# A two-block transformer on one core: the residual spilled to DRAM during the experts, and the second context stream woven in at 1.65 instead of 1.1

## The chip, the cores and the metric

The kernel runs on one core of one Trainium2 chip. The metric is the device time of one execution in microseconds (us): the median of three runs. The engines are named as the profile names them: PE (TensorE matmul), PEld (TensorE weight load), DVE (VectorE), ACT (ScalarE), POOL (GpSimd) and SP (SyncE, which only issues DMAs here).

## The reference

Two transformer blocks run one after the other on 512 latent tokens of width 1024. The first block ends in a mixture of experts, and the second block has two layers, each with its own context stream of 256 tokens. Cut to what matters:

```
# block 1
x = x + gt1 * token_mixer(...)                       # 512 x 1024
h2 = modulate(rms_norm(x, norm_ffn_g), sh2, sc2)
x = x + gt2 * hier_moe(h2)     # 32 experts, top-2 of 8 in the top-1 of 4 groups
x = rms_norm(x, final_norm_g)
# each expert: (silu(h @ w_gate) * (h @ w_up)) @ w_down, 1024 -> 512 -> 1024

# block 2, layer 0 and 1
for i in range(2):
    # keys and values of ctx_2 (256 tokens) and of x (512 tokens), three branches, merge, MLP
    x_new = x + gt1 * mix(x, ctx) + gt2 * squared_relu_mlp(...)
    if i == 0: ctx = ctx + ... mix_c ... + squared_relu_mlp(...)   # needs ctx_2 alone, not x
```

The context stream of layer 0 depends on `ctx_2` and on the second block's weights, and not on the output of the first block. It can therefore run beside the experts.

## The kernel before

All data are float32. Most products are made from high and low parts (`split`, L167 to L169: ACT writes the high part, DVE the low part) as three matmuls (L192, L193, L194). The experts use plain float32 matmuls instead (L1015 for gate and up, L1034 for down).

**Streams and weaving.** The parts of the program are Python generators that yield a number, an estimate of the work just laid down. `weave` steps the stream whose own time is lowest, and a stream's time advances by its number over its `speed`. A `main` stream has speed 1. The context path of layer 0, `path(0, 256)`, is in the list `ctx` and goes along behind several main streams: behind the last attention head, `project`, `route`, `experts` and `combine`. For the last two its speed is `CTX_SPEED`. What is left of it then runs alone (`drain(weave(ctx))` in `run`), and after that comes the latent path, `path(0, 512)`. Weaving sets the order of the program text, which is a priority: when the program is built, each engine's instructions are put in a fixed order from these priorities and from when operands and buffers were expected to be ready. On the chip each engine runs its list in that order.

**Numbers of the streams.** One pair of experts yields 4.2 + 4.2 + 4.2 + 0.5 = 13.1, and 16 pairs 209.6. `combine` yields 4 + 4 + 8 + 8 x 1.5 = 28. Of the context path, the steps still to come when the experts begin yield 354 in all, of which its MLP (the last part) is 163.2.

**The experts.** 32 experts are done as 16 pairs. A pair computes 64 rows of two experts: `gu` takes 8 rounds, first 4 of gate, then 4 of up, then `hr` and `hT`, then `py` in 4 rounds. Each round uses two weight tiles of 128 x 1024 (512 KB), one of each expert, in eight matmul instructions of 128x512, which use 64 columns of the array each. So a pair has 24 tiles and 96 instructions: 32 for gate, 32 for up, 32 for down. The tiles have the tag `wa`, of which there are 14 buffers (`WA`). `branch` starts the first `EARLY` tiles before the experts; every other tile is loaded where it is used in program order, as soon as a buffer is free. All these loads are issued by SP (L152), in one queue with the context path's weights (`wr`, 4 buffers `raw`, then 6 buffers `hl` for their high and low parts).

**The residual.** `project` writes the residual X, eight tiles of 128x512 in four `wa` buffers. `route` reads it for the router's norm. X then stays in these four buffers during the experts, so that 10 are left for expert weights. `combine` gathers the experts' rows from DRAM (`yr`, L1048), adds them to X (L1058), takes the sum of squares (`stat`, L235, L237, L241; `rms`, L248), scales X (L1066), stores it in `xs_dram[0]` (L1067) and prepares the sum of squares of the next norm, which opens `path(0, 512)`.

**Context MLP.** It has four quarters, and each quarter has 192 matmuls on `f` (first product) and 192 on `u` (second product), 1,536 in all, with 128x256 outputs.

Of the kernel before, what the change touches and what calls it, by code (L numbers as in the profile page):

```python
# [16 lines left out]
KD = 8  # L17
# [5 lines left out]
NONE = 4096  # L23
LAMBDA_INIT = 0.8 - 0.6 * math.exp(-0.3 * 0)
T2, WA, RAW, HL, AT = 35, 14, 4, 6, 9
EARLY = 8
CTX_SPEED = 1.1
MOD_SPEED = 0.4
PRIOR = 30
FIRST = 70.0  # L30
# [48 lines left out]
def weave(main, back=()):  # L79


    every = list(main) + list(back)
    for s in every:
        s.t = 0.0
    while any(not s.done for s in main) or any(s.hold for s in every):
        live = [s for s in every if not s.done]
        held = [s for s in live if s.hold]
        if held:
            live = [s for s in live if s.hold or not s.weights]
        if all(s.done for s in main):  # L90
            live = held
        yield abs(min(live, key=lambda v: v.t).step())


def drain(gen):
    for _ in gen:
        pass
# [7 lines left out]
class Gen:  # L105
# [252 lines left out]
    def run(self):  # L358
# [42 lines left out]
        if one:  # L401
            for gen, speed, held in ((project, PRO_SPEED, True), (self.route(), ROUTE_SPEED, False), (None, 0, 0),
                                     (self.experts(), CTX_SPEED, False), (self.combine(), CTX_SPEED, False)):
                if gen is None:
                    self.branch()
                    continue
                for s in ctx:
                    s.speed = speed
                drain(weave([Stream(gen, 1.0, held, (lambda: tc.high_priority(PRIOR)) if PRIOR and held is not None and speed != CTX_SPEED else None)], ctx))
        if two:  # L410
# [371 lines left out]
    def route(self):  # L782
        nc, A, tc = self.nc, self.A, self.tc
# [3 lines left out]
        X = self.X  # L787
# [11 lines left out]
        def ct(shape, name):  # L799
# [8 lines left out]
        ps = self.mm("lgT")  # L808
        yield from self.norm_mod(X, a2, b2, 512, h2, self.ss, lambda k: nc.tensor.matmul(
            ps[:36], wr[:, k, :], h2[k], start=k == 0, stop=k == KD - 1))  # L810
        lT = self.at("lgT")[:, :512]
        nc.vector.tensor_copy(lT[:36], ps[:36])
        ps = self.tp("lg")
# [133 lines left out]
    def branch(self):  # L947
# [4 lines left out]
        self.wq = []  # L952
        for _ in range(EARLY):
            self.next_weights()
# [83 lines left out]
            yield 0.5  # L1038

    def combine(self):  # L1040
        nc, X, ss = self.nc, self.X, []
        gf = self.const("final_norm_g")

        Y = []
        for t in range(4):
            rows = [self.wa("yr") for _ in range(2)]
            for j in range(2):
                nc.gpsimd.indirect_dma_start(out=rows[j], out_offset=None, in_=self.Yd[:, :],  # L1048
                                             in_offset=bass.IndirectOffsetOnAxis(ap=self.rows_at[:, 4 * j + t:4 * j + t + 1], axis=0))
            self.copy_act(rows[0], rows[0], scale=self.wt[:, 0, t:t + 1])  # L1050
            nc.vector.scalar_tensor_tensor(rows[0], rows[1], self.wt[:, 1, t:t + 1], rows[0], op0=OP.mult, op1=OP.add)
            Y.append(rows[0])
        yield 4
        for m in range(KD):
            ps = self.tp("yT")
            for t in range(4):
                self.tr(ps[:, t * P:(t + 1) * P], Y[t][:, m * P:(m + 1) * P])
            nc.vector.scalar_tensor_tensor(X[m], ps, self.gt2[:, m:m + 1], X[m], op0=OP.mult, op1=OP.add)  # L1058
            self.stat(ss, m, X[m], 512)
        del Y  # L1060
        yield 4
        r = self.spread(self.rms(ss, 512), 512)
        yield 8
        ss = []
        for m in range(KD):
            nc.vector.scalar_tensor_tensor(X[m], X[m], gf[:, m:m + 1], r, op0=OP.mult, op1=OP.mult)  # L1066
            nc.gpsimd.dma_start(self.xs_dram[0][m], X[m])  # L1067
            self.stat(ss, m, X[m], 512)
            yield 1.5
        self.ss = ss  # L1070
# [822 lines left out]
```

## Time and profile before

| | us |
|---|---|
| time, median of 3 runs | 3581.45 (3577.01 to 3581.93) |
| time of the profiled execution | 3592.64 |
| its span, first to last instruction | 3590.9 |
| first expert matmul | 614.8 |
| last expert matmul ends | 1369.4 |
| sum of squares that opens the latent path | 1551.1 |
| latent path's first norm complete | 1568 |

PE is busy 95% of the span, PEld 71%, DVE 47%, ACT 34% and POOL 10%. A PE slice lasts longer than the distance to the next one, because matmuls are pipelined. So a busy PE need not be a PE at its peak; the distance from one start to the next tells that. The DMA engines move 165 GB/s over the span, and some 330 GB/s during the experts.

### The profile page before, as it was taken

What the parts mean: (1) busy time and instruction counts of PE and PEld (TensorE: products, weight loads), DVE (VectorE), ACT (ScalarE), POOL (GpSimd) and SP (SyncE); (2) the same over time, 40 slices, a digit from 0 to 9 for tenths busy, and PEclk for the clock granted to TensorE, in tenths of its full rate; (3) what the DMA queues carried; (4) which work ended last, traced back from release to release, by engine and by line L of the source; (5) the groups of instructions that cost most, each with busy time, mean ns of one, the idle gap of its engine ahead of it and who ended that gap; (6) DMA issues with size and microseconds to landing.
All of it is one profiled execution on the core that took longest, in us unless ns stands there. A gap on an engine that the chain in (4) does not pass through costs nothing. (4 is left out here: it accounts for less than half of the span.)

```text
span 3590.9 us, 48889 instructions
## 1 busy us (share of the span) xinstructions
PE 3407.6 (95%) x19280; PEld 2545.7 (71%) x19280; DVE 1698.4 (47%) x3173; ACT 1234.3 (34%) x2194; POOL 341.7 (10%) x402
## 2 busy tenths in 40 slices
PE   7999998999999997999999999999999999999999
PEld 4977556555455446998567777888897777778887
DVE  5336535323322325654346746444555466644443
ACT  4214313323222213433335433333434344423332
POOL 1000001011111102110000112000200001020000
PEclk9999999999999998999999999999999899999999
DMA  7231566998889885543752223333433221132232
GB/s 262 85 126 36 187 224 239 348 363 339 318 322 351 314 291 217 186 136 105 242 174 71 61 68 107 99 119 117 138 106 105 79 79 60 37 123 83 94 100 82
DMA packets 195667, 591.84 MB, mean 165 GB/s; under 512 B 31867, under 2 KB 36731, under 8 KB 195436
## 3 DMA queue, kind: packets, MB, share of 16 engines
q1 hardware_dynamic: 177308, 537.55, 43.6%
q0 software_dynamic: 18128, 51.15, 3.9%
q8 instruction: 152, 2.49, 0.3%
q14 instruction: 79, 0.65, 0.1%
HBM read 561.59 MB, written 31.20 MB: 165 GB/s over the span
## 5 line engine op out<-in xcount | busy, mean ns | idle before, releaser
L169 DVE TENSOR_TENSOR wl<-wr,wh 128x1024 fp32r<-128x1024 f32 (+2 forms) x452 | 555.9, 1234 | 502.5 <-ACT wh L168 485.1
L168 ACT ACTIVATE wh<-wr 128x1024 fp32r<-128x1024 f32 (+2 forms) x452 | 471.9, 1048 | 665.1 <-PE mm L193 495.4
L192 PE MATMUL mm<-wh,h 128*128 128x256 f32 (+1 forms) x1104 | 323.9, 294 | 7.7 <-ACT h L277 4.3
L193 PE MATMUL mm<-wl,h 128*128 128x256 f32 (+1 forms) x1104 | 320.8, 291 | 0.0
L194 PE MATMUL mm<-wh,h 128*128 128x256 f32 (+1 forms) x1104 | 319.9, 291 | 0.2
L192 PE MATMUL mm<-f,wh 128*128 128x512 f32 (+1 forms) x768 | 276.6, 362 | 8.7 <-ACT wh L168 5.0
L1015 PE MATMUL gu<-we,xT 128*64 128x512 f32 x1024 | 283.3, 605 | 0.9 <-ACT xT L165 0.7
L192 PE MATMUL mm<-u,wh 128*128 128x512 f32 (+1 forms) x768 | 274.4, 358 | 5.2 <-ACT wh L168 5.0
L194 PE MATMUL mm<-f,wl 128*128 128x512 f32 (+1 forms) x768 | 276.8, 361 | 1.6 <-DVE wl L169 1.6
L194 PE MATMUL mm<-u,wl 128*128 128x512 f32 (+1 forms) x768 | 274.3, 358 | 3.6 <-DVE wl L169 3.6
L193 PE MATMUL mm<-f,wh 128*128 128x512 f32 (+1 forms) x768 | 275.8, 360 | 0.0
L193 PE MATMUL mm<-u,wh 128*128 128x512 f32 (+1 forms) x768 | 273.6, 357 | 0.0
L192 PEld LDWEIGHTS mm<-wh,h 128*128 128x128 f32 x1104 | 218.8, 198 | 22.3 <-issue 9.0
L194 PEld LDWEIGHTS mm<-wh,h 128*128 128x128 f32 x1104 | 218.3, 198 | 6.7 <-issue 4.7
L193 PEld LDWEIGHTS mm<-wl,h 128*128 128x128 f32 x1104 | 219.1, 199 | 2.9 <-issue 2.3
L192 PE MATMUL pg<-h,wh 128*128 128x512 f32 (+1 forms) x576 | 212.3, 369 | 7.2 <-ACT th L1715 4.8
L194 PE MATMUL pg<-h,wl 128*128 128x512 f32 (+1 forms) x576 | 209.0, 363 | 0.6 <-DVE wl L169 0.6
L193 PE MATMUL pg<-h,wh 128*128 128x512 f32 (+1 forms) x576 | 208.8, 363 | 0.0
L355 ACT ACTIVATE p<-S,mx 128x768 f32<-128x768 f32 (+2 forms) x192 | 144.6, 756 | 115.4 <-DVE mx L1422 62.3
L192 PEld LDWEIGHTS mm<-f,wh 128*128 128x128 f32 x768 | 148.6, 194 | 38.0 <-ACT wh L168 7.9
L194 PEld LDWEIGHTS mm<-f,wl 128*128 128x128 f32 x768 | 148.2, 193 | 33.3 <-issue 9.7
L192 PEld LDWEIGHTS mm<-u,wh 128*128 128x128 f32 x768 | 147.3, 192 | 29.0 <-ACT wh L168 7.6
(504 smaller groups left out, 6420.9 us busy)
## 6 DMA issues: line engine op xcount, KB each, us to landing
wr<-in_ffn_w_dram SPq DMA_DIRECT2D x192, 512.0 KB, 3.8
wr<-in_w_in_dram SPq DMA_DIRECT2D x178, 512.0 KB, 4.3
we<-in_expert_w_gate_dram SPq DMA_DIRECT2D x128, 512.0 KB, 6.8
we<-in_expert_w_up_dram SPq DMA_DIRECT2D x128, 512.0 KB, 7.3
we<-in_expert_w_down_dram SPq DMA_DIRECT2D x128, 512.0 KB, 7.2
wm<-in_w_mod_dram SPq DMA_DIRECT2D x96, 256.0 KB, 5.6
wm<-in_w_mod_dram SPq DMA_DIRECT2D x48, 512.0 KB, 4.8
wm<-in_w_ada_dram SPq DMA_DIRECT2D x64, 256.0 KB, 4.7
```

What stands on the lines that cost most here:

```text
L168: self.nc.scalar.activation(hi, src, AF.Copy)
L169: self.nc.vector.tensor_tensor(lo, src, hi.bitcast(F32), op=OP.subtract)
L192: mm(out, ah, bh, start=i == 0, stop=False)
L193: mm(out, ah, bl, start=False, stop=False)
L194: mm(out, al, bh, start=False, stop=i == n - 1)
L355: self.nc.scalar.activation(p, s, AF.Exp, bias=m, accum_out=sm)
L1015: nc.tensor.matmul(gu[64 * e:64 * e + 64, m * 512:m * 512 + 512], xT[k // 4][:, o:o + 64], w[e][kk], start=k == 0, stop=k == KD - 1)
```

## The change

`EARLY` becomes 12 and `CTX_SPEED` 1.65. At the end of the router's norm the eight tiles of X are stored to `xs_dram[0]` by POOL, and the program lets go of them, so that all 14 `wa` buffers are open to the experts. `combine` loads X again through SP into four `wa` buffers.

```diff
-EARLY = 8
-CTX_SPEED = 1.1
+EARLY = 12
+CTX_SPEED = 1.65
...
         yield from self.norm_mod(X, a2, b2, 512, h2, self.ss, lambda k: nc.tensor.matmul(
             ps[:36], wr[:, k, :], h2[k], start=k == 0, stop=k == KD - 1))
+        for m in range(KD):
+            nc.gpsimd.dma_start(self.xs_dram[0][m], X[m])
+        del X
+        self.X = None
...
     def combine(self):
-        nc, X, ss = self.nc, self.X, []
+        nc, ss = self.nc, []
+        X = self.X = self.load_x(self.xs_dram[0], 512, "xr", "wa")
```

## Rows read from the trace of the kernel before

**Rows 1.** The page's part 1: busy time, share, instructions of each engine.
```profile
PE 3407.6 (95%) x19280; PEld 2545.7 (71%) x19280; DVE 1698.4 (47%) x3173; ACT 1234.3 (34%) x2194; POOL 341.7 (10%) x402
```
**Rows 2.** Windows: length, each engine's busy time and count, PEclk, DMA share, GB/s.
```profile
613.00:1369.40 756.40, 717.59 (x3748) 390.11 (x3748) 223.80 (x468) 194.95 (x391) 95.16 (x128) 0.97 0.88 329
1369.40:1551.00 181.60, 163.05 (x1254) 159.60 (x1253) 120.54 (x166) 80.15 (x113) 37.58 (x37) 0.92 0.57 191
1551.00:1567.50 16.50, 10.42 (x62) 9.27 (x61) 14.22 (x30) 6.32 (x9) 2.70 (x5) 0.69 0.45 152
```
**Rows 3.** Timeline, PE: a whole block of 32, then 48 context matmuls.
```profile
629.38 7.09 PE L1015 MATMUL gu<-we,xT 128*64 128x512 f32 x32
636.40 0.39 PE L192 MATMUL mm<-h,wh 128*128 128x256 f32 x1
...
642.26 0.60 PE L208 MATMUL ht<-cc,hr 128*128 128x128 f32 x4
```
**Rows 4.** Timeline, PE: a block taken in pieces between context matmuls.
```profile
1262.39 1.93 PE L1034 MATMUL py<-we,hT 128*64 128x512 f32 x6
1264.25 0.39 PE L193 MATMUL mm<-f,wh 128*128 128x256 f32 x1
...
1265.16 1.07 PE L1034 MATMUL py<-we,hT 128*64 128x512 f32 x2
1266.16 0.38 PE L193 MATMUL mm<-f,wh 128*128 128x256 f32 x1
```
**Rows 5.** Timeline, PE: the first and the last burst of just two expert matmuls.
```profile
714.01 1.07 PE L1015 MATMUL gu<-we,xT 128*64 128x512 f32 x2
...
1338.99 1.07 PE L1015 MATMUL gu<-we,xT 128*64 128x512 f32 x2
```
**Rows 6.** Waits of SP's queue, 613 to 1369: us in total, times, longest.
```profile
SPq L152 <- PE gu L1015: 289.3, 155, 13.8
SPq L152 <- PE py L1034: 170.8, 59, 15.1
```
**Rows 7.** Waits of PE, 613 to 1369.
```profile
PE mm L192 <- ACT wh L168: 11.7, 9, 1.7
...
PE gu L1015 <- DMA we<-in_expert_w_gate_dram: 0.3, 1, 0.3
```
**Rows 8.** Windows: the stretch in which the DMAs moved most.
```profile
750.00:800.00 50.00, 48.26 (x280) 28.15 (x277) 11.03 (x14) 10.80 (x16) 4.26 (x6) 1.00 0.99 377
```
**Rows 9.** Windows with one tile, PE alone: `f`, the context MLP's first product.
```profile
613.00:1369.40 756.40, 31.00 (x192) 0.97 0.88 329
```
**Rows 10.** The same for `u`, the second product.
```profile
613.00:1369.40 756.40, 22.05 (x144) 0.97 0.88 329
```
**Rows 11.** Timeline, all engines: the links of `combine` and the next norm.
```profile
1374.73 1.02 POOL L1048 DMA_INDIRECT yr<-Yd,cc  x1 [3.11 <-issue]
...
1396.08 1.28 DVE L1051 SCALAR_TENSOR_TENSOR yr<-yr,cc,yr 128x1024 f32<-128x1024 f32 x1
...
1413.54 0.59 PE L248 MATMUL ss<-cc,sq 128*128 128x1 f32 x2 [6.53 <-POOL sq L241]
...
1424.11 0.75 DVE L1066 SCALAR_TENSOR_TENSOR xr<-xr,cc,rb 128x512 f32<-128x512 f32 x1 [0.79 <-PE rb L208]
...
1441.89 0.73 DVE L1066 SCALAR_TENSOR_TENSOR xr<-xr,cc,rb 128x512 f32<-128x512 f32 x1
...
1551.10 1.84 PE L248 MATMUL ss<-cc,sq 128*128 128x1 f32 x16
```
**Rows 12.** Timeline, POOL: the idle stretch before the first store of the router's rows.
```profile
561.53 0.58 POOL L824 DMA_DIRECT2D Hd<-h2r  x1 [42.92 <-ACT h2r L165]
```
**Rows 13.** The page's part 6: DMAs, KB each, median us from issue to landing.
```profile
xres<-xr POOLq DMA_DIRECT2D x16, 256.0 KB, 3.4
xr<-xres SPq DMA_DIRECT2D x16, 256.0 KB, 5.3
```

## The prediction

> **What bounds the kernel now.** I read the page's busy times first, then windows by stage, then PE's timeline inside the experts. PE is busy 95% of the span [rows 1], so the question is where its time isn't work. The stage of the experts lasts 756.4 us with PE busy 717.6 us of them, but PEld only 390 us [rows 2]. The distances between starts tell more. A whole block of 32 expert matmuls takes 636.40 - 629.38 = 7.02 us, 0.219 us each, and the 48 context matmuls behind it take 5.86 us, 0.122 us each [rows 3]. At these paces the 1,536 expert matmuls (16 pairs of 96) need 337 us, and the other 3748 - 1536 = 2,212 need 270 us. That is 607 us; 149 us of the stage are lost.
>
> Where they go is seen in the second timeline. A round of eight expert matmuls is often cut in two and six, because one tile of the round was expected later than the other. The two halves of the array then don't work side by side: six take 1264.25 - 1262.39 = 1.86 us, two take 1.00 us [rows 4], and eight in a whole block 1.75 us. With the context run that is started once more between them (six matmuls in 0.91 us instead of 0.73), a cut costs 2.86 - 1.75 + 0.18 = 1.29 us. There are 52 bursts of exactly two in the stage, none before 714 us [rows 5], so cuts cost some 67 us. PE's clock stands at a mean of 0.97 in the stage [rows 2], which at its two levels means 45 us at 1.2 GHz and 23 us lost. The rest is the ends of short bursts and waits of PE for the high parts of context weights, the largest group 11.7 us; expert weights are hardly ever waited for, 0.3 us [rows 7].
>
> Why were the tiles expected late? SP waited 289 + 171 us for PE to free buffers [rows 6], so the ten buffers set how far ahead loads can run. The stage moved 329 GB/s x 756.4 us = 249 MB; at the paces above, in 607 us, it would need 410 GB/s. The busiest 50 us that I found in this stage moved 377 [rows 8]. So at full pace weights can't keep up, and the order was laid around that.
>
> The Trainium skill, Perfetto Trace Analysis, section Identifying the Most-Contended Engine, says that matmul busy time misjudges headroom and that LDWEIGHTS busy should be used. By the busy row, 95%, context work moved into the stage would lengthen it one for one and save nothing else, so that the sum below would end at +19 us; by the LDWEIGHTS row, 52%, there is room. The trace sides with the page, by the 149 us.
>
> **The change, part by part.**
> 1. *Context work moves.* When the experts begin, 354 units of the context path are left. Before, the experts take 209.6 x 1.1 = 231 of them, and 123 stay, three quarters of the MLP. After, they take 209.6 x 1.65 = 346 and 8 stay. The trace follows the text closely: 192 + 144 = 336 MLP matmuls lie in the stage [rows 9, 10], where the text puts a quarter, 384; 48 lag. So 1,200 came later. After, 8 units are 76 matmuls, and with the same lag 124 come later: 1,076 move. At 0.122 us they add 131 us to the stage.
> 2. *The stretch behind the experts shrinks.* From the last expert matmul to the sum of squares that opens the latent path it is 181.6 us [rows 2]. With no context left, the chain of `combine` sets it: 28.0 us to the last row sum (1369.4 to 1397.4), 16.1 to the first sum of squares, 10.6 to the first scaling, and 18.5 of scaling in which DVE also split context weights [rows 11], then up to 5 us of POOL's sums: 79 us as it stands. Without the context's work on DVE, ACT and POOL I estimate 64; eight scalings of 0.74 and four squares of 0.7 are 9 us, and POOL's six sums and eight stores, which lag, some 15. I take 70. So 181.6 - 70 = 112 us go (103 to 118). The 124 matmuls left, 15 us, fit into its idle time. The 16.5 us of the first latent norm [rows 2] are paid before and after.
> 3. *Fewer cuts.* Demand at full pace falls, since context work brings fewer bytes per PE time than experts: a half chunk, 0.52 MB, per 24 matmuls adds 1076 / 24 x 0.52 = 23.5 MB, less 2 MB loaded earlier. 270 MB over 607 + 131 = 738 us is 366 GB/s, now under the 377 seen [rows 8]. And 14 buffers instead of ten let SP load six tiles into the next block while a block of eight is used. So most cuts should go: from 52 to about 10, -54 us. Bounds: none (0) and all (-67). Of the 82 us of other losses (clock, waits for context weights queued on SP behind expert loads that wait for a buffer, short bursts) I take 12 back; bounds 0 and 41.
> 4. *The spill.* POOL issues eight stores; a store of its own kind takes 0.54 to 0.58 us to issue, so 4.5 us. They stand before the stores of the router's rows, where POOL was idle for 42.9 us [rows 12]. Free; without that cover 4.5 us, and the gathers of the first experts would be late by that. They need X alone, so buffers come free when the norm has read X, as 2 MB land (3.4 us each [rows 13]).
> 5. *The reload.* SP issues eight loads, 5.3 us to landing [rows 13], behind the last expert loads and before the remaining context weights and the latent path's first ones. They wait for buffers that the last expert blocks free, and for the spill, long done. X is first needed behind the gathers, 27 us after the last expert matmul [rows 11]. Free; uncovered 5 to 10 us.
> 6. *Twelve early tiles.* Four more loads of 512 KB stand on SP before context weights that PE uses while the router ends: at 377 GB/s 1.4 us each, up to 5.6 us late. Against that, second-block tiles land sooner, up to 1.6 us. Taken as 0, bounds -2 and +6.
>
> The sum: +131 - 112 - 54 - 12 = -47 us on 3592.6 us, the profiled execution. The stage would last 756 + 131 - 66 = 821 us, above its floors of 738 (PE) and 270 / 377 = 716 (memory). The median of the runs lies 11.2 us under the profiled execution; the same -47 on 3581.45 gives **3534 us**.
>
> A rule that speaks against the change: the Trainium skill, TensorEngine Tiling (Array Packing), Key Properties, says that changing the tiling mode drains the engine. Expert matmuls use half-width tiles and context matmuls the whole array, so each change of hand would cost. The row says how little: 32 expert matmuls and the change behind them take 7.02 us [rows 3], at most 0.2 us over the pace of pairs. With 0.56 us as the drain, what a short burst exceeds the block's pace by, 48 whole blocks would lose 18 us more, and the sum would be -29.
>
> **The rivals.**
> *A. The cover runs out (slower).* `combine` is a chain of gathers, small sums and scalings in which PE has little to do. Before, 1,200 context matmuls lay over it and behind it. If cuts stay as many as now, the stage takes all of the 131 us, and the price is +131 - 112 = +19 us, at 3600. It decides if fewer than 15 cuts go away. For it: PE's mean clock was 0.92 there even with context work [rows 2], and bare it would be lower at the start of the latent path, some 4 us. Against: there were no cuts before 714 us, so they aren't in the nature of the weave.
> *B. Cuts grow with the context steps (slower).* Half again as many steps per expert step could be half again as many cuts, 78: +34 us and in all +53, at 3634. The pieces of six in the MLP [rows 4] speak for it, the lower demand against.
> *C. Half of it (no change).* If 366 GB/s can't be held throughout, since 377 was one stretch, the gain pays just for the bare `combine`: about 15 cuts go, 3575 to 3588. The same holds if the freed buffers bring nothing, because X's are let go too late or the queue of SP is held elsewhere.
>
> **How the numbers follow.** Forecast 0.67, A 0.14, B 0.05, C 0.14. The forecast's own range is the bounds of steps 2 and 3 about the sum: from +131 - 118 - 67 - 41 = -95 to a gain of 10 us, 3486 to 3571. A measurement can tell about 0.2%, 7 us, from no change. So faster 0.67, same 0.14, slower 0.19. The range leaves out B, the far end of A and the forecast's last tenth: 3493 to 3598.
>
> **What would show it.** In the windows: the experts' stage about 821 us long, 1,410 of 1,536 context MLP matmuls in it, PE and DMA at 330 GB/s; behind it about 70 us instead of 182 to the sum of squares, with PE idle for most. In PE's timeline: expert blocks of 32 and 24, few bursts of two. In the waits: SP still on PE, PE not on expert weights. I am wrong if bursts of two are as many as now, if PE waits for expert weights, or if the stretch behind the experts stays over 90 us.

## The result and the profile after

The changed kernel takes 3545.88 us (median of 4 runs, 3538.35 to 3547.45), against 3580.62 for the kernel before. The ratio is 0.990, 95% interval 0.9883 to 0.9918, so 29 to 42 us were won. The forecast was 3534.

The busy times of the page, in answer to [rows 1]:

```profile
PE 3357.0 (95%) x19280; PEld 2533.0 (71%) x19280; DVE 1693.2 (48%) x3173; ACT 1234.2 (35%) x2194; POOL 340.3 (10%) x410
```

The windows of after, in answer to [rows 2]: first to last expert matmul, from there to the sum of squares that opens the latent path, and the 15.7 us behind that.

```profile
616.90:1439.10 822.20, 795.71 (x4796) 505.44 (x4796) 302.76 (x580) 255.50 (x481) 92.89 (x130) 0.98 0.89 332
1439.10:1504.30 65.20, 32.96 (x197) 29.50 (x197) 37.41 (x56) 18.98 (x22) 33.10 (x37) 0.71 0.53 194
1504.30:1520.00 15.70, 11.37 (x56) 10.38 (x56) 10.48 (x25) 4.08 (x6) 2.01 (x4) 0.58 0.22 67
```

The stage grew to 822 us, and the stretch behind it fell from 181.6 to 65.2. In the stretch PE is busy for half of the time. The tiles of the context MLP in the stage, in answer to [rows 9, 10], `f` first, then `u`:

```profile
616.90:1439.10 822.20, 101.98 (x768) 0.98 0.89 332
616.90:1439.10 822.20, 86.85 (x624) 0.98 0.89 332
```

So 768 + 624 = 1,392 of its 1,536 matmuls lie in the stage, where 336 did. Most expert blocks in it are whole now; some rounds are still cut, as the four matmuls here are (timeline of PE; the edit moves L1015 to L1019 and L1034 to L1038), in answer to [rows 3, 4, 5]:

```profile
800.75 7.09 PE L1038 MATMUL py<-we,hT 128*64 128x512 f32 x32
...
819.45 1.08 PE L1019 MATMUL gu<-we,xT 128*64 128x512 f32 x4
```

The chain of `combine` as PE sees it (timeline of after, in a view that opens inside the last expert block; the brackets hold the idle time and what ended it), in answer to [rows 11]:

```profile
1435.45 3.60 PE L1038 MATMUL py<-we,hT 128*64 128x512 f32 x16
1458.77 0.44 PE L208 MATMUL yT<-cc,yr 128*128 128x128 f32 x2 [2.91 <-DVE yr L1056]
...
1477.06 0.66 PE L208 MATMUL yT<-cc,yr 128*128 128x128 f32 x4 [0.27 <-DVE xr L1063]
1483.79 3.58 PE L248 MATMUL ss<-cc,sq 128*128 128x1 f32 x16 [6.07 <-POOL sq L241]
1489.89 1.09 PE L208 MATMUL rb<-cc,rs 128*128 128x128 f32 x4 [2.53 <-DVE rs L221]
1504.26 3.57 PE L248 MATMUL ss<-cc,sq 128*128 128x1 f32 x16 [13.29 <-POOL sq L241]
```

PE now waits for the links of the chain, 13.29 us for the last sum of POOL. The waits of SP's queue in after between 616 and 1436, in answer to [rows 6]:

```profile
SPq L152 <- PE gu L1019: 227.4, 102, 9.2
SPq L152 <- DVE wl L169: 112.5, 31, 13.0
SPq L152 <- PE py L1038: 98.1, 37, 11.6
```

SP still waits most for PE. Its wait for the low parts of context weights (`wl`) grew from 12.1 to 112.5 us, with more context weights in the queue. PE has no wait for expert weights left in the stage (0.3 us before [rows 7]).

**Where the time went.** For every run of PE matmuls of one kind in the stage I took the time from its first start to the next kind's first start, less 0.219 us for each expert matmul and 0.122 for each other (the paces of [rows 3]). What is left over is "lost"; a "burst of two" is a run of exactly two expert matmuls. The kernels below before and after are those of the experiments. "Stage" runs from the first start to the last end of an expert matmul here, so that before has 754.6 us instead of the 756.4 of its window [rows 2]:

| kernel | ratio to before (95%) | stage | context matmuls in it | bursts of two | lost by expert / context bursts | lost in all | stretch behind |
|---|---|---|---|---|---|---|---|
| before | 1 | 754.6 | 2,020 | 52 | 82 / 62 | 149 | 181.7 |
| after | 0.990 (0.9883 to 0.9918) | 822.2 | 3,076 | 13 | 42 / 43 | 88 | 65.2 |
| buffers alone (1.1) | 0.998 (0.9965 to 0.9995) | 746.3 | 2,020 | 51 | 80 / 58 | 141 | 179.7 |
| pace alone (1.65) | 0.992 (0.9903 to 0.9942) | 823.2 | 3,076 | 13 | 46 / 41 | 89 | 70.0 |
| after, four buffers held | 0.989 (0.9871 to 0.9907) | 821.3 | 3,076 | 13 | 42 / 43 | 87 | 66.5 |
| after at 1.5 | 0.988 (0.9859 to 0.9896) | 799.6 | 2,788 | 26 | 58 / 40 | 101 | 80.6 |
| before, half loads | 0.970 (0.9684 to 0.9724) | 647.1 | 2,029 | 8 | 12 / 27 | 41 | 176.6 |
| before, turned | 0.978 (0.9758 to 0.9795) | 673.2 | 2,020 | 4 | 23 / 37 | 68 | 178.9 |
| after, turned | 0.979 (0.9771 to 0.9812) | 787.2 | 3,076 | 0 | 10 / 39 | 53 | 62.8 |
| after at 1.5, turned | 0.976 (0.9741 to 0.9779) | 760.4 | 2,788 | 2 | 20 / 37 | 61 | 81.6 |
| after at 1.3, turned | 0.976 (0.9738 to 0.9773) | 711.5 | 2,404 | 0 | 14 / 39 | 59 | 127.8 |
| before at 1.5, turned | 0.978 (0.9756 to 0.9794) | 772.6 | 2,788 | 3 | 26 / 44 | 74 | 82.3 |

From before to after, 1,056 x 0.122 = 129 us came into the stage, 61 us of losses left it, and the stretch gave 116. That is 48 us between the two profiled executions; the medians lie 35 apart.

Part of what is lost is PE's clock and not the order. The granted clock, averaged over the stage from the trace's own record, is 0.973 before, 0.982 after, 0.980 with the buffers alone and 0.985 in the turned kernel. As the missing share of the stage, that is 20 us before, 15 after, 15 and 10.

### The profile page after: what moved, and what is told of

It is laid out like the page before. It is cut to its first block, busy times and chain, and to the rows that moved or that the text cites. A ratio compares the mean times of both kernels' runs of the same rounds, so it can differ in the third digit from the quotient of the medians.

```text
span 3542.7 us, 48935 instructions
## 1 busy us (share of the span) xinstructions
PE 3357.0 (95%) x19280; PEld 2533.0 (71%) x19280; DVE 1693.2 (48%) x3173; ACT 1234.2 (35%) x2194; POOL 340.3 (10%) x410
## 5 line engine op out<-in xcount | busy, mean ns | idle before, releaser
L1019 PE MATMUL gu<-we,xT 128*64 128x512 f32 x1024 | 251.7, 601 | 0.7 <-ACT xT L165 0.7
L194 PEld LDWEIGHTS mm<-u,wl 128*128 128x128 f32 x768 | 147.4, 193 | 25.5 <-DVE wl L169 4.7
```

Of the source, the lines that this page charges most:

```text
L194: mm(out, al, bh, start=False, stop=i == n - 1)
L1019: nc.tensor.matmul(gu[64 * e:64 * e + 64, m * 512:m * 512 + 512], xT[k // 4][:, o:o + 64], w[e][kk], start=k == 0, stop=k == KD - 1)
```

## The experiments

**The kernel before once more**, with a profile.

> The kernel before, unchanged, for a second profiled execution. The profiled one of before lay 11 us above the median of its runs, and the medians of before and after lie 35 us apart where the two profiled executions lie 48 apart. If those 11 us are an accident of that execution inside the experts' stage, the stage is 745 us here instead of 756, with some 43 bursts of two instead of 52. If they lie elsewhere (start, latent path, end), the stage is 756 us again and the 52 bursts with it. The time itself should be 3581 within 0.2%.

Measured: 3581.61 us (8 runs), ratio 1.0002, interval 0.9987 to 1.0017. The profiled execution has a stage of 754.4 us with 52 bursts of two, a stretch of 180.0, and a span of 3585.2 us. So the stage repeats to 0.2 us, with the same 52 bursts. The extra time of the first profiled execution isn't in the stage: 4 of the 6 us between the two spans lie behind the sum of squares (2034.1 against 2030.0 us to the last matmul).

**The buffers alone.** Against after:

```diff
-CTX_SPEED = 1.65
+CTX_SPEED = 1.1
```

> After with the context at 1.1 steps per expert step as before: X is spilled and reloaded, 14 buffers and 12 early tiles serve the experts, but no context work moves. My theory (cuts come from loads that can't keep up at full pace, 410 GB/s wanted against 377 seen, and buffers only help to ride it out): cuts fall from 52 to some 35, -22 us, time near 3558. Rival, the buffers do it all: cuts fall to the 13 of after, -50 us and -12 of other losses, time 3520 to 3530. Rival, the context's pace does it all: 52 cuts stay, 3580. Stretch behind the experts 182 us in each case.

Measured: 3574.46 us, ratio 0.998. The window of the stage:

```profile
611.30:1357.60 746.30, 711.72 (x3740) 384.64 (x3740) 222.88 (x468) 191.82 (x389) 96.54 (x128) 0.98 0.89 334
```

51 bursts of two against 52: four more buffers take away one cut. Losses fell by 8 us, half of it in context bursts; 5 of the 8 lie in the clock (20 us lost to it before, 15 here). My 35 cuts were wrong, and the rival of the pace was right, but for 2 to 13 us.

**The pace alone.** Against before:

```diff
-CTX_SPEED = 1.1
+CTX_SPEED = 1.65
```

> Before with 1.65 context steps per expert step: X stays in its eight halves of buffers, ten buffers for the experts. 1,076 context matmuls move (+131 us in the stage), the stretch behind falls by some 115 us. My theory (demand falls to 366 GB/s, below the 377 seen): cuts fall to some 25, -35 us, time 3560 to 3570. Rival, the buffers do it all: 52 cuts stay or grow, +16 to +19, time about 3600. Rival, the pace does it all and the spill is idle: as after, 3546.

Measured: 3551.95 us, ratio 0.992; 13 bursts of two, as in after. Stage and stretch:

```profile
613.80:1436.90 823.10, 794.75 (x4796) 504.57 (x4796) 302.53 (x580) 255.23 (x481) 94.93 (x130) 0.99 0.89 330
1436.90:1507.00 70.10, 31.22 (x199) 28.19 (x197) 38.34 (x56) 18.86 (x22) 34.17 (x37) 0.73 0.51 180
```

Without any spill the losses are 89 us, in after 88. So the pace brings most of the change: 28 of 35 us by the medians, and the intervals of 0.992 and 0.990 overlap.

**Four buffers held.** Against after:

```diff
-EARLY = 12
+EARLY = 8
...
     def experts(self):
+        hold = [self.wa("hold") for _ in range(4)]
+        for t in hold:
+            nc.gpsimd.memset(t[:, :1], 0.0)
```

and the four tiles are let go at the end of `experts`.

> After with X spilled and reloaded and 1.65 steps, but eight early tiles instead of twelve, and four of the 14 buffers held by unused tiles throughout the experts, so that ten serve them as before. It parts the spill from what the freed buffers bring. If the freed buffers bring nothing (bursts of two were 51 with them at 1.1 and 13 without them at 1.65): as the run with the pace alone, 3546 to 3552, and spill and reload free. If they bring the 7 us that the run with the buffers alone gained: 3552. If the spill costs something that the buffers pay for: over 3555.

Measured: 3543.82 us, ratio 0.989. Stage 821.3 us against 822.2, losses 87 against 88. At this pace the freed buffers and the twelve early tiles bring nothing that can be seen, and spill and reload cost nothing that can be seen. Against the pace alone, 0.992, this kernel even lies lower; the intervals just overlap, and stage and stretch together take 887.8 us against 893.3. Whether the early store of X itself wins these few us stays open.

**After at 1.5 steps.** Against after:

```diff
-CTX_SPEED = 1.65
+CTX_SPEED = 1.5
```

> After with 1.5 instead of 1.65 context steps per expert step. Some 209.6 x 0.15 = 31 units of the context path, about 300 matmuls or 37 us, stay for the stretch behind the experts, where PE was all but idle for 65 us in after. If what bounds that stretch is the chain of combine alone, and context matmuls lie beside it for nothing: stage 37 us shorter, stretch 65 to 75 us, time 3510 to 3520. Rival: the context's steps on DVE, ACT and POOL lengthen the chain by as much, or cuts come back with the higher demand (380 GB/s): no better than after, 3546, stretch about 100 us.

Measured: 3534.51 us, ratio 0.988. The stretch:

```profile
1412.00:1492.60 80.60, 67.26 (x487) 64.05 (x486) 61.65 (x86) 35.42 (x49) 35.11 (x37) 0.87 0.62 217
```

Both sides were partly right. 288 matmuls leave the stage (-35 us), the stretch grows by 15 us instead of at most 10, and cuts come back, 26 instead of 13, with 13 us of losses. By the traces 7 us are left, by the medians 11.

**Half loads.** Each expert weight tile loads only its first 512 columns and uses them for both halves. Against before:

```diff
-        w = self.load(self.wa("we"), self.A["expert_w_" + m][e, q])
-        self.wq.append([w[:, :512], w[:, 512:]])
+        w = self.load(self.wa("we")[:, :512], self.A["expert_w_" + m][e, q][:, :512])
+        self.wq.append([w, w])
```

> Before, but each expert weight tile loads only the first 512 of its 1024 columns and uses them for both halves, so the experts' bytes are halved and their matmuls stay as they are (the output is another one). If rounds are cut because the order was laid around weights that can't come at full pace (memory), the 52 bursts of two nearly vanish and the stage loses 1.29 us for each, 55 to 65 us: time 3515 to 3525. If they come from the number of buffers or from the weave's steps, which are as before, 52 stay and the time is 3575 to 3580.

Measured: 3476.80 us, ratio 0.970.

```profile
610.30:1257.40 647.10, 637.22 (x3751) 372.55 (x3750) 225.43 (x471) 197.42 (x392) 92.22 (x128) 0.99 0.72 235
```

With ten buffers and 1.1 steps as before, 8 bursts of two are left of 52, and 41 us of losses of 149. So the cuts come from the bytes that the experts want, not from the number of buffers or the steps of the weave. PE hardly waits for expert weights before the change (0.3 us [rows 7]): what fewer bytes alter is when a tile is expected, and the order that is laid by it. It went 40 us beyond what I expected. Whole blocks came with it: all bursts of experts together lose 12 us instead of 82, and of the 108 us of losses that went, 13 are clock (0.988 against 0.973).

**The turned order.** Against before, in `gu` and in `py`:

```diff
-                        for e in range(2):
+                        for e in (1, 0):
```

> Before with nothing moved, but within a round the matmuls take the second expert's tile first, the one that is loaded later. A round can then no longer be cut into two and six. It measures the price of a cut by itself. By the 1.29 us of the forecast 48 to 52 cuts fewer are worth 62 to 67 us, and the time would be 3515 to 3520. Rival: the two matmuls before the cut filled time in which PE would otherwise wait for the second tile, so that the wait moves ahead of the whole round and shows as PE's wait for expert weights: nothing gained, 3575 to 3585. If the loss of a cut is the restart of the context run alone (0.18 us each), 9 us, 3570.

Measured: 3507.20 us, ratio 0.978. The stage, and the timeline of PE with one round:

```profile
616.40:1289.50 673.10, 649.19 (x3741) 369.91 (x3741) 227.16 (x469) 197.06 (x390) 93.63 (x128) 0.98 0.96 370
```

```profile
1261.09 1.94 PE L1015 MATMUL gu<-we,xT 128*64 128x512 f32 x8
1262.95 0.39 PE L192 MATMUL mm<-u,wh 128*128 128x256 f32 x1
...
1264.36 0.28 PE L194 MATMUL mm<-u,wl 128*128 128x256 f32 x1
1264.57 1.94 PE L1015 MATMUL gu<-we,xT 128*64 128x512 f32 x8
```

All eight matmuls of a round take 1262.95 - 1261.09 = 1.86 us. In [rows 4] six of them took 1.86 and the other two 1.00 on top. The wait didn't move ahead of the round; PE waits for gate tiles for 2.2 us in the whole stage:

```profile
PE gu L1015 <- DMA we<-in_expert_w_gate_dram: 2.2, 3, 1.1
```

Losses fall by 81.5 us for 48 bursts of two fewer, 1.70 us each: 1.23 in expert bursts, 0.54 in context bursts, and transposes 0.07 the other way. I had taken 1.29. The 1.70 isn't the price of a cut alone, though: 10 of the 81.5 us are clock (20 us lost to it before, 10 here). Of the 23 us that context matmuls without transposes lose less, 8 lie where the clock was at its lower level, 10 at the first and last matmuls of bursts, 5 between.

**After at 1.5, turned.** Against after:

```diff
-CTX_SPEED = 1.65
+CTX_SPEED = 1.5
...
-                        for e in range(2):
+                        for e in (1, 0):
```

> After with 1.5 steps and the second expert's tile first: the 26 bursts of two that the run with 1.5 still had go as well. At 1.29 us each that is 34 us below its 3534.5: 3500. If the price of a cut is the restart alone, 3530. If whole rounds wait for the later tile instead, 3534 or more, with PE's waits for expert weights grown by as much.

Measured: 3496.26 us, ratio 0.976. Two bursts of two instead of 26, and 39 us of losses fewer than at 1.5 alone, 1.64 each. The first side, 3500, was right to 4 us, with the price again above 1.29.

**After, turned.** The turned order alone, against after:

```diff
-                        for e in range(2):
+                        for e in (1, 0):
```

> After with the second expert's tile first, so that neither kernel has cuts to win: the change, seen on top of the turned order. With 52 fewer bursts the turned kernel before stood at 3507 (stage 673 us, 1.70 us for each of 48 cuts). My theory: the change gains by cuts alone, and the moved work itself is rival A's sum, +131 in the stage and -113 behind it. So the turned kernel is slower with the change than without it: 3507 + 18 = 3525, or from after: 3546 - 13 x 1.70 = 3524. Rival: the change gains by something else as well (buffers, clock, waits); then it is 3507 or below.

Measured: 3508.33 us, ratio 0.979, where the turned kernel without the change has 0.978.

```profile
617.30:1404.50 787.20, 771.77 (x4797) 495.64 (x4797) 304.57 (x581) 256.78 (x482) 90.27 (x130) 0.99 0.93 348
1404.50:1467.30 62.80, 31.90 (x196) 28.43 (x196) 37.33 (x55) 18.03 (x21) 33.32 (x37) 0.70 0.53 193
```

On whole rounds the change gains nothing, as my theory had it, but it doesn't cost 18 us either: my 3525 was wrong, and the rival's 3507 right within the noise. The moved work costs 129 - 116 = 13 us, and the losses fall by 15, mostly because expert bursts lose 10 us instead of 23. The turned kernel loses 12.7 us in distances of more than 1 us behind an expert matmul, such as the two waits of 2.26 us for `hr` (L1022); with the change there is none. So the gain that isn't cuts looks like waits that more context work covers, about as much as the move costs.

**After at 1.3, turned.** Against after:

```diff
-CTX_SPEED = 1.65
+CTX_SPEED = 1.3
...
-                        for e in range(2):
+                        for e in (1, 0):
```

> After with 1.3 steps and the second expert's tile first. Some 816 context matmuls stay behind the experts (432 at 1.5, 1,200 at 1.1). If the stretch behind the experts shrinks by 0.127 us for each matmul that leaves it, as between those two (179 us with 1,200, 82 with 432), and the stage grows by 0.122 us for each, the pace makes no difference between 1.1 and 1.5: 3496 to 3507. Rival: the higher pace itself helps the stage (other losses fall from 66 to 60 us), 3502. Rival: at 1.3 the bytes wanted, some 395 GB/s at full pace, are the bound as at 1.1, 3507.

Measured: 3494.20 us, ratio 0.976; the stretch is 127.8 us where 0.127 us for each matmul gave 131. The first side, 3496 to 3507, was right but for 2 us: between 1.3 and 1.5 the pace makes no difference, and the interval of the turned kernel at 1.1 overlaps too. With the turned kernel at 1.5 this is the fastest that computes the same, 1.5% below after (3494.20 / 3545.88).

**Before at 1.5, turned**: no spill, ten buffers. Against before:

```diff
-CTX_SPEED = 1.1
+CTX_SPEED = 1.5
...
-                        for e in range(2):
+                        for e in (1, 0):
```

> Before with 1.5 steps and the second expert's tile first: no spill, no reload, ten buffers, eight early tiles. If the spill and the freed buffers bring nothing here either, as at 1.65: 3496 within 0.3%. If the freed buffers matter now that rounds are whole and loads run at their fastest (370 GB/s in the turned kernel): 3503 to 3510, with more waits of PE for expert weights.

Measured: 3503.32 us, ratio 0.978 (0.9756 to 0.9794) against 0.976 (0.9741 to 0.9779) with the spill. The intervals overlap. The profiled stage is 12 us longer, 772.6 against 760.4 us, with losses of 74 against 61. PE's wait for expert weights is 1.0 us, and 6 of the 13 us of losses are clock (0.980 against 0.988). Whether the freed buffers help whole rounds stays open.

## Why the prediction was right, point by point

**The mechanism was right in outline:** work moves into the stage, the stretch behind shrinks, and cuts pay for it. The stage was put at 821 us (822.2 measured; counted as in the table it grew by 67.6 us where 65 were forecast), the opening of the latent path by the sum of -47 at 1504 (1504.3), some 1,410 MLP matmuls in the stage (1,392), 330 GB/s there (332). PE doesn't wait for expert weights, and 28 bursts of 32 and 3 of 24 are left among 95 bursts, where before has 19 and 8 among 159. By its own signs of being wrong it stands.

**Step 1, +131:** 1,056 matmuls moved instead of 1,076. At 0.122 us that is +129. The 144 left fit into the stretch.

**Step 2, -112:** measured 181.7 - 65.2 = 116 us gone, inside the bounds. From the first scaling to the sum of squares, put at 15, it takes 13.2 us (1491.09 to 1504.26), all of it inside PE's wait of 13.29 for POOL; the links before that, put at 55, take 52. (The links of before add up to 78 us, not 79.) The first scaling, in DVE's timeline of after:

```profile
1491.09 2.06 DVE L1071 SCALAR_TENSOR_TENSOR xr<-xr,cc,rb 128x512 f32<-128x512 f32 x3 [1.35 <-PE rb L208]
```

**Step 3, -54 and -12:** the sum of -66 was nearly right (-61), and 13 bursts of two were left where 10 were forecast. Its parts were not. First, the reason: it named the lower demand and the 14 buffers. Half the bytes with ten buffers remove 44 of the 52 bursts of two, 14 buffers without the higher pace remove one. So the demand decides, and the buffers belong out of the step. That the higher pace acts by lowering the demand fits both runs; it isn't shown by itself. Second, the price: 1.29 us per cut is too small for what goes away with a cut, 1.70 by the turned order. The expert part is 1.23 where 1.11 were taken, and the context part 0.54 where 0.18 were. That a restart itself costs more than 0.18 isn't shown, as 10 us at the ends of context bursts for 48 cuts are 0.2 each, and the clock has a good part of the rest. At 1.70, 39 cuts are 66 us and leave nothing for "other losses", yet 5 of the 61 us are clock, so how the 61 part into cuts and others stays open. That the two parts of step 3 add up so nearly is partly luck. And a price per burst of two is itself rough: from after to its turned kernel 13 fewer go with 35 us, since rounds there are cut in other ways too (46 expert bursts of under eight in after, 16 in the turned one; 110 and 16 for before).

**Steps 4 and 5, free:** no cost is seen, by the pace alone (0.992 without the spill, 0.990 with it) and by the held buffers (0.989). The cover named in step 4 wasn't the one used. POOL's timeline has the stores between the sums of squares, and the long idle stretch is still there, in answer to [rows 12]:

```profile
499.83 0.56 POOL L812 DMA_DIRECT2D xres<-xr  x1 [12.03 <-DVE xr L761]
500.41 1.30 POOL L241 TENSOR_TENSOR sq<-sq,sq 128x512 f32<-128x512 f32 x1
...
563.27 0.54 POOL L828 DMA_DIRECT2D Hd<-h2r  x1 [41.15 <-ACT h2r L165]
```

The reload is issued before the last expert matmuls, and X is first used 32 us behind them (SP's and DVE's timelines):

```profile
1426.54 6.81 SPq L152 DMA_DIRECT2D xr<-xres  x8
```

```profile
1471.07 1.41 DVE L1063 SCALAR_TENSOR_TENSOR xr<-yT,cc,xr 128x512 f32<-128x512 f32 x2 [0.57 <-PE yT L208]
```

**Step 6, 0:** with eight early tiles and the buffers held, the first expert matmul comes at 612.8 us, with twelve in after at 616.9. The kernels before, with eight, have 614.8 and 615.2, and the buffers alone, with twelve, 611.3. The sign changes within this scatter, so no effect is seen.

**From the profile to the median** is where the 12 us between forecast and result arose. The sum of -47 agrees with the traces: from the first expert matmul to the opening of the latent path it is 936.3 us before and 887.4 after, -49. But I took the 11.2 us by which one profiled execution lay above the median as a constant. The second profiled execution of before lies 5 us above its median, that of after 1 us below. Over the thirteen profiled kernels and executions, the first expert matmul comes between 608.6 and 617.3 us, and the stretch from the opening of the latent path to the last matmul, where all have the same source, takes 2030.0 to 2037.2. So one profiled span says little about the median to within some 8 us in either direction. The spans of the second execution of before and of after differ by 42.5 us, at the end of the interval of the medians (29 to 42); why the medians differ less than the traces isn't settled further.

**The rivals.** A's condition, fewer than 15 cuts gone, didn't come (39 went). Its price of +19 for the moved work was near: 129 - 116 = 13 us in the traces. On whole rounds as much is won back by losses, and the change comes out even (0.979 against 0.978). The forecast's own range left this to A: by the bounds of steps 2 and 3 it would end at +131 - 103 = 28 us slower, and it was cut at a gain of 10. B's 78 cuts didn't come; the run with the pace alone has 13. C said that the gain fails if the freed buffers bring nothing. At 1.65 they bring nothing that can be seen, and the gain came all the same.

**What the forecast overlooked** is the cheaper remedy. It read the cut of two and six as the price of late weights, while it takes late weights and an order within the round: the expert whose tile is loaded first also went first, so its two matmuls could start alone. Turning that order gains 76 us by the medians without moving anything, twice what the change gained, and leaves the change nothing to win.

## What to carry to other kernels

Count the runs of matmuls of each kind on PE and what each loses against the pace of a whole block, before moving work: here 149 us of a 755 us stage were lost to cut rounds, restarts, waits and clock, 81.5 of them went with a turned loop, and PE's busy share of 95% showed none of it. Where two tiles share the array side by side, let the one that arrives last go first in the order, so that a group starts only when it is whole. An edit with several parts (spill, buffers, early loads, pace) should be run part by part: here the pace did most of it, and what spill and buffers add at that pace is too little to be told from noise.

## What the runs showed that was not expected

Six matmuls of a round that follow a cut take 1.86 us [rows 4], as long as all eight of an uncut round with context matmuls on either side (1.86 in the turned kernel). The two ahead of the cut are pure loss, 1.00 us. The single starts in the trace show why. The six of [rows 4] start at 1262.389, 1262.395, 1262.869, 1262.875, 1263.298 and 1263.727: two pairs side by side, then two of the second expert with no partner left. The eight of the turned round start in four pairs, at 1261.087, 1261.567, 1261.996 and 1262.425 with the partner 6 or 7 ns behind. Both take four steps of 0.42 to 0.53 us, and the two ahead of a cut add two more steps, 0.48 and 0.52 in 49 of the 52 bursts of two.

The DMAs carried more than thought: 370 GB/s as the mean of a stage of 673 us in the turned kernel, with a DMA share of 0.96, where 377 was the best 50 us of before [rows 8]. So on whole rounds the stage stands close to its loads.

The bare stretch behind the experts, with a granted clock of 0.71 and then 0.58, cost the latent path nothing that can be seen: from its opening to the last matmul it takes 2032.5 us in after, and 2034.1 and 2030.0 in the two executions of before.
